# Storing the two halves of each weight next to each other, word by word, so that a weight load steps over every second word

## The chip, the cores and the metric

One NeuronCore of a Trainium2 chip runs the whole program in one launch. The time is device microseconds of one execution. The engines are named as the profile names them: PE is TensorE's matmul stream, PEld its weight loads, DVE is VectorE, ACT is ScalarE, POOL is GpSimd, SP the engine that issues DMAs.

## What is computed

Three blocks in a row on 256 tokens of width 1024: two layers of (feed-forward, a mixer of three recurrent kinds, feed-forward), and a block with attention, a convolution and a feed-forward with a convolution in it. Nearly all arithmetic is in dense products `x @ w` in float32; cut to what matters here:

```python
def swiglu(x, w_gate_up, w_down):                      # widths 1024 -> 2 x 2816 -> 1024
    gate, up = jnp.split(x @ w_gate_up, 2, axis=-1)
    return (jax.nn.silu(gate) * up) @ w_down
...
x = x + FFN_HALF * swiglu(rms_norm(x, g1), ...)        # first feed-forward of a layer
x = x + mixers(rms_norm(x, g2) @ w_in) @ w_out         # ssd, mlstm, rwkv heads
x = x + FFN_HALF * swiglu(rms_norm(x, g3), ...)        # second feed-forward of a layer
...
x = x + gt1 * (mixed @ w_out)                          # last block: attention and convolution
x = x + gt2 * ((silu(gte) * val) @ w_down)             # last block: feed-forward
```

## The kernel before, in words

All weights of the dense products lie in DRAM as one stream `ws` of 3,808 blocks of 128 x 128 in the order in which they are used, 7 blocks to a chunk (`CB`), 544 chunks. A chunk passes through three steps. `fetch` (lines 121 to 124) loads it with one DMA into a `raw` tile (128 x 896 float32, 6 buffers). `chunk` (lines 126 to 136) lets ACT round it into a tile `whi` of the type fp32r (line 134), and lets DVE subtract the rounded value from the raw one into a second tile `wlo` (line 135); each has 4 buffers. `mm` (lines 151 to 155) then does three matmuls for every block: rounded weights by rounded activations (153), rounded weights by the activations' remainder (154), remainder of the weights by rounded activations (155). Weights are the side that is loaded into the array, 128 columns; the streamed side is 256 tokens (258 in the first groups of the last block). So there are 3 x 3,808 = 11,424 dense matmuls, each with a weight load of its own, and a chunk serves 21 of them.

The activations are kept as two fp32r tiles as well: `pair0` and `pair1` (16 KB a partition, halves 8 KB apart) for inputs of width 1024, `hp` for the inner width of a feed-forward, `xg` for two groups that start before a norm is known. `split` (lines 204 to 206) makes them with the same two operations.

A feed-forward (`ffn`, line 321 on) is 22 steps of two output tiles of 8 blocks each (gate and up), and then the down projection over 22 blocks for each of 8 output tiles. On the profile's clock the five down projections run at about 136 to 195, 598 to 657, 782 to 845, 1242 to 1305 and 1550 to 1615 us, the gate and up parts before them at 23 to 136, 486 to 598, 670 to 781, 1131 to 1242 and 1436 to 1550 us (the last one with a convolution, `taps3`, after each product). Between 195 and 486 and between 845 and 1131 us stand the mixers, with many small float32 matmuls, and from 1305 to 1436 us attention.

The order of instructions on each engine is made by a scheduler from the order in which the code issues them and from priorities; the weight copies have a high one (`tc.high_priority(AHEAD)`). Semaphores follow from the tiles: the first matmul on a chunk waits for ACT, the third for DVE, ACT waits until a buffer is no longer read.

`gap` (lines 258 to 261) allocates a tile that nothing reads and has POOL fill it; its only effect is to move the tiles that are allocated after it. `GAPS` (line 41) holds its sizes in bytes a partition. With them, in the built program, every `whi` and `wlo` buffer begins at byte 416 of a 512-byte period (a block is 512 bytes wide, so every block does), `pair0` at 96, `pair1` at 352, and the five `hp` tiles, in the order of the down projections above, at 96, 352, 160, 32 and 288.

Three more lines are named below. Line 221 is the sum over channels for a norm: weights 128 x 128, one streamed column. Line 671 is an ACT pass of 256 elements that reads a tile once by columns (a step of 64 bytes) and once by rows; line 617 a DVE pass of 256 elements that writes with a step of 128 bytes. Lines 1215 and 1216 are float32 matmuls of attention, 64 weight columns and 128 streamed ones, in two passes each.

Of the kernel before, what the change touches and what calls it, by code (L numbers as in the profile page):

```python
# [8 lines left out]
F32 = mybir.dt.float32  # L9
F32R = mybir.dt.float32r  # L10
# [17 lines left out]
CB = 7  # L28
NB = 4
# [8 lines left out]
GD_AHEAD = 1  # L38
BOOST = (1, 1, 1, 1, 1)
DENSE = 0.34  # L40
GAPS = {"xg": 448, "xn": 192, "mix": 288, "ffn": (384, 128, 448, 192, 448), "attn": 256}
W_OUT = ((("rwkv0", "rwkv1"), (12, 13, 14, 15)), (("ssd",), (0, 1, 2, 3, 4, 5, 6, 7)), (("mlstm",), (8, 9, 10, 11)))

IN_PAIRS = "k0 r0 v0 r2 k2 v2 xb8 xb0 dtg xb2 xb4 xb6 z0 z2 z4 xm0 z6 xm2 o0 o2".split()
# [33 lines left out]
def _program(tc, a, order, dbg=None):  # L78
# [3 lines left out]
    V, S, G, PE = nc.vector, nc.scalar, nc.gpsimd, nc.tensor  # L82

    def pool(name, bufs=1, **kw):
        return es.enter_context(tc.tile_pool(name=name, bufs=bufs, **kw))

    const = pool("const")
    wp = pool("weights")
# [30 lines left out]
    chunks, raws = {}, {}  # L119

    def fetch(ci):
        if ci not in raws and ci < N_CHUNKS:
            raws[ci] = wp.tile([128, CB * 128], F32, name="raw", bufs=NR)
            nc.sync.dma_start(raws[ci], a["ws"][ci])

    def chunk(ci):
        if ci in chunks or ci >= N_CHUNKS:
            return
        fetch(ci)
        raw = raws[ci]  # L130
        hi = wp.tile([128, CB * 128], F32R, name="whi", bufs=NB)
        lo = wp.tile([128, CB * 128], F32R, name="wlo", bufs=NB)
        with tc.high_priority(AHEAD):
            S.copy(hi, raw)  # L134
            V.tensor_sub(lo, raw, hi.bitcast(F32))  # L135
        chunks[ci] = (hi, lo)

    def block(mat, l, k, m):
        i = len(order)
        order.append((mat, l, k, m))  # L140
        ci, b = divmod(i, CB)
        for c in range(ci, ci + NB):
            chunk(c)
        for c in range(ci, ci + NR):
            fetch(c)
        hi, lo = chunks[ci]
        if b == CB - 1:
            del chunks[ci - 1 if ci - 1 in chunks else ci]
        return hi[:, b * 128:b * 128 + 128], lo[:, b * 128:b * 128 + 128]
# [92 lines left out]
    def stat_rstd(accs, width, eps, chain=False):  # L242
# [9 lines left out]
            S.copy(rb, p2[:, i * T:(i + 1) * T])  # L252
            out.append(rb)
        return out

    turn = []

    def gap(pool, n):
        if n:
            turn.append(0)  # L260
            G.memset(pool.tile([128, n // 4], F32, name=f"gap{len(turn)}"), 0.0)

    pairs = []

    def pair(dtype=F32R):
        pairs.append(0)
        return act.tile([128, 2, DT, T], dtype, name=f"pair{len(pairs) % 2}")
# [4 lines left out]
    def new_acc():  # L272
        return act.tile([128, 2, T], F32, name="acc", bufs=2)
# [47 lines left out]
    def ffn(l, which, acc, xg, next_gain):  # L321
        with tc.tile_pool(name=f"ffn{which}{l}", bufs=1) as fp:
            gu, dn = f"ffn{which}_w_gate_up", f"ffn{which}_w_down"
            gap(fp, GAPS["ffn"][2 * l + which - 1])
            hp = fp.tile([128, 2, FT, T], F32R, name="hp")
            rb, = stat_rstd([acc], D, EPS)
# [58 lines left out]
    def mixers(l, acc, xg):  # L385
# [6 lines left out]
        def weight(i):  # L392
            w = ring(128, 512)
            nc.sync.dma_start(w, a["small"][l, i])
            return w

        gap(mp, GAPS["mix"])
        nka = mp.tile([128, 4], F32, name="nka")
        V.tensor_scalar(nka, P(f"k_a{l}", 0, 4), -1.0, None, op0=OP.mult)
# [739 lines left out]
    def modulate(rb, gain, shift):  # L1139
        xn = pair()  # L1140
        for j in range(DT):
            n = tmp()[:, 0]
            V.scalar_tensor_tensor(n, x[:, j], gain[:, j:j + 1], rb, op0=OP.mult, op1=OP.mult)
            S.activation(xn[:, 0, j], n, AF.Identity, bias=shift[:, j:j + 1])
            V.scalar_tensor_tensor(xn[:, 1, j], n, shift[:, j:j + 1], xn[:, 0, j].bitcast(F32),
                                   op0=OP.add, op1=OP.subtract)
        return xn
# [12 lines left out]
    def second(accs, xg):  # L1160
        rb, rb2 = stat_rstd(accs, D, EPS, chain=True)
        with tc.tile_pool(name="attn", bufs=1) as mp:
            xn = modulate(rb2, a1[:, 0], mod[:, 0:8])
            gap(mp, GAPS["attn"])
            mixed = [mp.tile([128, 2, 4, T], F32R, name=f"m{i}") for i in range(2)]
            at, cv = (mp.tile([128, 4, T], F32, name=n) for n in ("at", "cv"))
# [101 lines left out]
        with tc.tile_pool(name="ffn_2", bufs=1) as fp:  # L1268
            rb, = stat_rstd([acc], D, EPS)
            xn = modulate(rb, a1[:, 1], mod[:, 24:32])  # L1270
            gap(fp, GAPS["ffn"][4])
            hp = fp.tile([128, 2, FT, T], F32R, name="hp")
# [40 lines left out]
    acc = new_acc()  # L1313
    gap(act, GAPS["xg"])
    xg = pair()
    gap(act, GAPS["xn"])
    for j in range(0, DT, 2):
        nc.sync.dma_start(x[:, j:j + 2], a["xT"][:, j:j + 2])
        gained((j, j + 1), xg, "ffn1_norm0")
        chunk(j // 2)  # L1320
# [6 lines left out]
    for l in range(LAYERS):  # L1327
        acc, xg = ffn(l, 1, acc, xg, f"mix_norm{l}")
        dbg(f"xa{l}", x)
        acc, xg = mixers(l, acc, xg)  # L1330
# [4 lines left out]
        acc, xg = ffn(l, 2, acc, xg, f"ffn1_norm{l + 1}" if l + 1 < LAYERS else None)  # L1335
# [162 lines left out]
```

## Time and profile before

| what | value |
|---|---|
| median of 2 runs | 1624.52 us (1621.25 to 1627.79) |
| the profiled execution | 1627.1 us |
| its span, first to last instruction | 1625.3 us |
| mean granted clock of TensorE | 0.989 |
| busy share PE, PEld, DVE, ACT, POOL | 98%, 93%, 71%, 62%, 3% |
| DMA: HBM read, mean rate over the span | 287.51 MB, 178 GB/s |

Busy shares count an engine as busy while any row of it runs. Matmul rows are pipelined: a row lasts from its issue to the end of its last column, and the next begins before that, so the share of PE says that matmuls follow each other without a pause, and not how fast they follow. The pace is read from start times in the timeline, or from the number of matmuls in a stretch. The windows view gives for a stretch, from the span's start in us, the busy time of each engine and the number of its instructions that overlap the stretch (x), the granted clock of TensorE as a share of 2.4 GHz, and the DMA engines' share and rate.

### The profile page before, as it was taken

Reading aid. Unit: us, or ns where it says so; the run is one execution under the profiler, and the core shown is the slowest. Engines: PE = TensorE matmul, PEld = TensorE weight load, DVE = VectorE, ACT = ScalarE, POOL = GpSimd, SP = SyncE. Lnnn points to the kernel's source line nnn. Section 1 sums busy time; section 2 is a strip of 40 time slices with the busy share of each in tenths; the row PEclk is TensorE's granted clock in tenths of the full one; section 3 lists DMA queues with packets and bytes.
Section 4 is the critical chain, followed back from the end, with each engine's and each line's share of the span. In section 5 each row is a group of like instructions: output and inputs, shape, how many; then the busy total and the mean of one; then the engine's idle time right before and its main releaser. Section 6 shows DMA issues by size and latency. Waiting matters only on the chain.

```text
span 1625.3 us, 33775 instructions
## 1 busy us (share of the span) xinstructions
PE 1584.9 (98%) x13660; PEld 1516.4 (93%) x13660; DVE 1161.4 (71%) x1965; ACT 1000.1 (62%) x1692; POOL 47.5 (3%) x68
## 2 busy tenths in 40 slices
PE   8999999999999999999999899999999999999998
PEld 7999988878999999999998887799999998999997
DVE  7865679856787755787568975688785676798853
ACT  6554576887655454545458788765554566587753
POOL 0000001000000000000000100000000000000000
PEclk9999989999999999999999999999999999999999
DMA  7866633333357766597563333436886653556662
GB/s 252 306 195 190 204 118 123 101 112 116 115 181 244 242 187 194 185 329 260 183 194 125 115 106 117 127 117 216 288 306 185 185 166 113 159 162 190 187 189 72
DMA packets 106717, 290.81 MB, mean 179 GB/s; under 512 B 15640, under 2 KB 28096, under 8 KB 106432
## 3 DMA queue, kind: packets, MB, share of 16 engines
q1 hardware_dynamic: 106272, 288.12, 55.9%
q8 instruction: 107, 1.75, 0.4%
q10 hardware_dynamic: 288, 0.52, 0.1%
q14 instruction: 50, 0.41, 0.1%
HBM read 287.51 MB, written 1.09 MB: 178 GB/s over the span
## 4 chain that ended last, share of the span: by engine, by line
PE 77%; issue 13%; DVE 5%; ACT 2%; DMA 1%; POOL 1%; SPq 0%; DVEq 0%; POOLq 0%; ACTq 0%
PE d L155 21%; PE d L153 21%; PE d L154 21%; DVE wlo L135 1%; DMA ada<-ada 1%; PE m L691 1%; PE m L754 1%; PE m L1064 1%; POOL stm L212 1%; PE m L1068 1%; PE m L736 1%; PE st L221 1%; PE m L705 1%; ACT whi L134 1%; PE m L1066 1%
## 5 line engine op out<-in xcount | busy, mean ns | idle before, releaser
L135 DVE TENSOR_TENSOR wlo<-raw,whi 128x896 fp32r<-128x896 f32 x544 | 590.4, 1089 | 245.1 <-ACT whi L134 242.3
L153 PE MATMUL d<-pair,whi 128*128 128x256 f32 x2672 | 753.2, 282 | 4.8 <-ACT whi L134 2.1
L155 PE MATMUL d<-pair,wlo 128*128 128x256 f32 x2672 | 753.8, 282 | 1.8 <-DVE wlo L135 1.8
L154 PE MATMUL d<-pair,whi 128*128 128x256 f32 x2672 | 752.9, 282 | 0.1
L134 ACT CAST whi<-raw 128x896 fp32r<-128x896 f32 x544 | 511.5, 943 | 348.3 <-PE d L154 254.0
L153 PEld LDWEIGHTS d<-pair,whi 128*128 128x128 f32 x2672 | 508.8, 190 | 14.8 <-issue 5.9
L155 PEld LDWEIGHTS d<-pair,wlo 128*128 128x128 f32 x2672 | 508.1, 190 | 7.2 <-DVE wlo L135 2.9
L154 PEld LDWEIGHTS d<-pair,whi 128*128 128x128 f32 x2672 | 508.5, 190 | 3.0 <-issue 1.4
L154 PE MATMUL d<-hp,whi 128*128 128x256 f32 x880 | 246.6, 280 | 0.0
L155 PE MATMUL d<-hp,wlo 128*128 128x256 f32 x880 | 246.1, 280 | 0.0
L153 PE MATMUL d<-hp,whi 128*128 128x256 f32 x880 | 246.1, 280 | 0.0
L155 PEld LDWEIGHTS d<-hp,wlo 128*128 128x128 f32 x880 | 166.2, 189 | 0.0
L154 PEld LDWEIGHTS d<-hp,whi 128*128 128x128 f32 x880 | 166.1, 189 | 0.0
L153 PEld LDWEIGHTS d<-hp,whi 128*128 128x128 f32 x880 | 166.1, 189 | 0.0
L205 ACT CAST hp<-h 128x256 fp32r<-128x256 f32 x88 | 35.4, 406 | 90.9 <-DVE h L345 90.8
L1124 DVE SCALAR_TENSOR_TENSOR adasum<-ada,sc,adasum 128x1024 f32<-128x1024 f32 x42 | 53.8, 1281 | 14.4 <-DMA ada<-ada 14.4
L206 DVE TENSOR_TENSOR hp<-h,hp 128x256 fp32r<-128x256 f32 x88 | 36.7, 421 | 15.3 <-ACT hp L205 14.5
L1157 DVE SCALAR_TENSOR_TENSOR up<-raw,par,up 128x255 f32<-128x255 f32 (+1 forms) x88 | 37.2, 480 | 10.6 <-ACT raw L1153 10.3
L344 ACT ACTIVATE s<-d 128x256 f32<-128x256 f32 x80 | 30.2, 378 | 23.3 <-PE d L155 22.2
L345 DVE TENSOR_TENSOR h<-s,d 128x256 f32<-128x256 f32 x88 | 36.0, 415 | 3.8 <-ACT s L344 3.8
L155 PE MATMUL d<-w,wlo 128*128 128x256 f32 x128 | 37.1, 290 | 0.0
L154 PE MATMUL d<-w,whi 128*128 128x256 f32 x128 | 37.1, 290 | 0.0
(403 smaller groups left out, 1829.0 us busy)
## 6 DMA issues: line engine op xcount, KB each, us to landing
raw<-ws SPq DMA_DIRECT2D x544, 448.0 KB, 3.7
ada<-ada SPq DMA_DIRECT2D x48, 512.0 KB, 5.9
w<-da SPq DMA_DIRECT2D x16, 256.0 KB, 5.1
w<-small SPq DMA_DIRECT2D x10, 256.0 KB, 3.9
ab<-abias SPq DMA_DIRECT2D x1, 1536.0 KB, 7.1
x<-xT SPq DMA_DIRECT2D x4, 256.0 KB, 4.9
w<-da SPq DMA_DIRECT2D x8, 128.0 KB, 3.6
w<-dw SPq DMA_DIRECT2D x4, 256.0 KB, 5.5
```

Of the source, the lines that this page charges most:

```text
L134: S.copy(hi, raw)
L135: V.tensor_sub(lo, raw, hi.bitcast(F32))
L153: PE.matmul(p, h, xh, start=start, stop=False, skip_group_check=True)
L154: PE.matmul(p, h, xl, start=False, stop=False, skip_group_check=True)
L155: PE.matmul(p, lo, xh, start=False, stop=stop, skip_group_check=True)
L205: S.copy(hi, src)
L206: V.tensor_sub(lo, src, hi.bitcast(F32))
L212: G.tensor_tensor(dst, m, mhalf.to_broadcast([128, n]), op=OP.pow)
L344: S.activation(s, p[:, 0], AF.Silu)
L345: V.tensor_mul(h, s, p[:, 1])
L1124: V.scalar_tensor_tensor(acc, w, sc[:, k:k + 1], acc, op0=OP.mult, op1=OP.add)
L1157: V.scalar_tensor_tensor(dst[:, i, d:], raw[:, i, :T - d], P(w, 3 * j + k), dst[:, i, d:], op0=OP.mult, op1=OP.add)
```

## The change

The two tiles `whi` and `wlo` of a chunk become one tile `wsp` of 128 x 896 x 2: word 0 of each pair is the rounded value, word 1 the remainder. `hi` and `lo` are views of it with a step of two words (8 bytes). ACT and DVE write through these views, DVE reads `hi` through one, and the weight loads read them. A buffer has 7,168 bytes, as the two had together, and there are 4 as before. The sizes of the gap tiles are other ones, and there is a new gap ahead of the first weight buffer; `gap` itself moves up in the code without a change.

```diff
-GAPS = {"xg": 448, "xn": 192, "mix": 288, "ffn": (384, 128, 448, 192, 448), "attn": 256}
+GAPS = {"w": 96, "xg": 64, "xn": 64, "mix": 32, "ffn": (0, 64, 192, 0, 64), "attn": 0}
...
     def chunk(ci):
         if ci in chunks or ci >= N_CHUNKS:
             return
         fetch(ci)
         raw = raws[ci]
-        hi = wp.tile([128, CB * 128], F32R, name="whi", bufs=NB)
-        lo = wp.tile([128, CB * 128], F32R, name="wlo", bufs=NB)
+        if not chunks:
+            gap(wp, GAPS["w"] * (not order))
+        w = wp.tile([128, CB * 128, 2], F32R, name="wsp", bufs=NB)
+        hi, lo = w[:, :, 0], w[:, :, 1]
         with tc.high_priority(AHEAD):
             S.copy(hi, raw)
             V.tensor_sub(lo, raw, hi.bitcast(F32))
```

In the built program every `wsp` buffer begins at a multiple of 1,024 bytes, and a block is 1,024 bytes wide. In the 512-byte period `pair0` now begins at 192, `pair1` at 64, and the five `hp` tiles at 320, 384, 0, 448 and 0. Each engine has as many instructions as before, but POOL, which fills two gap tiles fewer. The scheduler orders a few of them otherwise. Lines 126 to 262 stand 9 further down in the new file, later ones 2.

On DVE, in the gate and up part of the last feed-forward (1436 to 1550 us before), L135 is the subtraction for a chunk, L1157 the convolution, L1287 the product of the two halves, L206 the remainder of the activations. Before:

```order
1438 L135 TENSOR_TENSOR wlo<-raw,whi 128x896
1439 L206 TENSOR_TENSOR hp<-up,hp 128x256
1440 L1157 SCALAR_TENSOR_TENSOR up<-raw,par,up 128x255 x2
1441 L1157 SCALAR_TENSOR_TENSOR up<-raw,par,up 128x254 x2
1442 L135 TENSOR_TENSOR wlo<-raw,whi 128x896
1443 L1287 TENSOR_TENSOR up<-up 128x256
1444 L135 TENSOR_TENSOR wlo<-raw,whi 128x896
1445 L206 TENSOR_TENSOR hp<-up,hp 128x256
1446 L135 TENSOR_TENSOR wlo<-raw,whi 128x896
```

And now, at the same place (L144 is L135, L215 L206, L1159 L1157, L1289 L1287):

```order
1442 L144 TENSOR_TENSOR wsp<-raw,wsp 128x896
1443 L215 TENSOR_TENSOR hp<-up,hp 128x256
1444 L1159 SCALAR_TENSOR_TENSOR up<-raw,par,up 128x255 x2
1445 L1159 SCALAR_TENSOR_TENSOR up<-raw,par,up 128x254 x2
1446 L144 TENSOR_TENSOR wsp<-raw,wsp 128x896 x2
1447 L1289 TENSOR_TENSOR up<-up 128x256
1448 L144 TENSOR_TENSOR wsp<-raw,wsp 128x896
1449 L215 TENSOR_TENSOR hp<-up,hp 128x256
```

One subtraction for a coming chunk moves ahead of the product of the halves by three places; the number of each kind is the same. On POOL, from the program's start, the gap tiles are filled in the same places (`gap` and the number of a tile; L212 is the root of a norm). Before:

```order
6 L261 MEMSET gap_88 128x112
7 L261 MEMSET gap_91 128x48
8 L261 MEMSET gap_153 128x96
9 L212 ISA
10 L212 TENSOR_TENSOR stm<-stm,mhalf 128x2
11 L261 MEMSET gap_2471 128x72
```

Now:

```order
6 L131 MEMSET gap_88 128x16
7 L131 MEMSET gap_91 128x16
8 L131 MEMSET gap_100 128x24
9 L221 ISA
10 L221 TENSOR_TENSOR stm<-stm,mhalf 128x2
11 L131 MEMSET gap_2392 128x8
```

The fills are smaller; the third one is that ahead of the weight buffers, where that of the first feed-forward stood.

## Rows read from the trace of the kernel before

**Rows 1.** The page: busy us, share of the span, instructions.
```profile
PE 1584.9 (98%) x13660; PEld 1516.4 (93%) x13660; DVE 1161.4 (71%) x1965; ACT 1000.1 (62%) x1692; POOL 47.5 (3%) x68
```
**Rows 2.** The page: the chain that ended last, by engine and by line.
```profile
PE 77%; issue 13%; DVE 5%; ACT 2%; DMA 1%; POOL 1%; SPq 0%; DVEq 0%; POOLq 0%; ACTq 0%
PE d L155 21%; PE d L153 21%; PE d L154 21%; DVE wlo L135 1%; DMA ada<-ada 1%; PE m L691 1%; PE m L754 1%; PE m L1064 1%; POOL stm L212 1%; PE m L1068 1%; PE m L736 1%; PE st L221 1%; PE m L705 1%; ACT whi L134 1%; PE m L1066 1%
```
**Rows 3.** Timeline of PEld, 137.0 to 137.6 us: start us, length us, instruction.
```profile
136.98 0.19 PEld L154 LDWEIGHTS d<-hp,whi 128*128 128x128 f32 x1
137.09 0.19 PEld L155 LDWEIGHTS d<-hp,wlo 128*128 128x128 f32 x1
137.21 0.19 PEld L153 LDWEIGHTS d<-hp,whi 128*128 128x128 f32 x1
```
**Rows 4.** Timeline of PE, same stretch.
```profile
136.98 0.28 PE L153 MATMUL d<-hp,whi 128*128 128x256 f32 x1
137.09 0.28 PE L154 MATMUL d<-hp,whi 128*128 128x256 f32 x1
137.21 0.28 PE L155 MATMUL d<-hp,wlo 128*128 128x256 f32 x1
```
**Rows 5.** Timeline of PEld, 16.1 to 17.0 us.
```profile
16.17 0.98 PEld L221 LDWEIGHTS st<-ones,acc 128*128 128x128 f32 x8
```
**Rows 6.** Timeline of PE, 1372.0 to 1372.8 us.
```profile
1372.11 0.38 PE L1215 MATMUL m<-sT,vn 128*64 128x128 f32 x2
1372.33 0.38 PE L1216 MATMUL m<-sT,vn 128*64 128x128 f32 x2
```
**Rows 7.** Windows: stretch, its length, busy us (x count) by engine, clock, DMA.
```profile
23.00:136.00 113.00, 111.73 (x978) 110.36 (x977) 79.99 (x110) 58.70 (x94) 0.00 (x0) 1.00 0.73 237
136.00:195.00 59.00, 59.00 (x523) 59.00 (x522) 34.83 (x42) 28.78 (x38) 0.00 (x0) 1.00 0.63 195
670.00:781.00 111.00, 110.97 (x979) 109.64 (x978) 84.66 (x113) 57.18 (x93) 0.00 (x0) 1.00 0.79 267
782.00:845.00 63.00, 63.00 (x528) 63.00 (x527) 34.90 (x42) 29.01 (x39) 0.00 (x0) 1.00 0.59 183
1242.00:1305.00 63.00, 63.00 (x533) 63.00 (x533) 37.39 (x47) 31.54 (x46) 0.00 (x0) 1.00 0.61 184
1436.00:1550.00 114.00, 113.54 (x964) 113.33 (x963) 100.81 (x185) 89.95 (x162) 0.00 (x0) 1.00 0.60 185
1550.00:1615.00 65.00, 65.00 (x543) 64.16 (x542) 32.58 (x42) 28.29 (x40) 0.00 (x0) 1.00 0.42 128
...
441.00:461.00 20.00, 20.00 (x174) 20.00 (x173) 13.25 (x17) 8.99 (x12) 2.47 (x1) 1.00 0.55 168
```
**Rows 8.** Lines L671, L617 and L206: shortest, median, longest ns.
```profile
L671 ACT ACTIVATE w<-w,cst x16: 493/622/759, 280.5 to 976.2; 128x256 f32<-128x256 f32 x16
...
L617 DVE TENSOR_TENSOR w<-am,cst x16: 577/601/631, 249.3 to 929.4; 32x256 f32<-32x256 f32 x16
...
L206 DVE TENSOR_TENSOR hp<-h,hp x88: 415/420/428, 32.0 to 1245.6; 128x256 fp32r<-128x256 f32 x88
```
**Rows 9.** The page: groups of instructions, busy us, mean ns, idle time before them.
```profile
L135 DVE TENSOR_TENSOR wlo<-raw,whi 128x896 fp32r<-128x896 f32 x544 | 590.4, 1089 | 245.1 <-ACT whi L134 242.3
...
L134 ACT CAST whi<-raw 128x896 fp32r<-128x896 f32 x544 | 511.5, 943 | 348.3 <-PE d L154 254.0
```
**Rows 10.** Waits: who waited for whom, us in total, times, longest us.
```profile
ACT whi L134 <- PE d L154: 254.0, 203, 5.0
```

More of the change, by code (lines that the diff above doesn't have):

```diff
@@ L124, in fetch, with gap @@
             nc.sync.dma_start(raws[ci], a["ws"][ci])
+    turn = []
+    def gap(pool, n):
+        if n:
+            turn.append(0)
+            G.memset(pool.tile([128, n // 4], F32, name=f"gap{len(turn)}"), 0.0)
     def chunk(ci):
@@ L254, in stat_rstd @@
         return out
[L256 to L261, printed above, removed]
     pairs = []
```

## Prediction

> **What bounds the kernel now.** I read the page's busy shares first: the matmul row of TensorE (PE) covers 98% of the span, VectorE (DVE) 71%, ScalarE (ACT) 62% [rows 1]. The chain that ended last agrees: 77% of the span is PE, the three matmul lines of `mm` are the first three entries with 21% each, and the DVE pass that makes the remainder half appears with 1% [rows 2]. So the rate of the 11,424 dense matmuls (3 for each of 3,808 weight blocks) is the time, and all else matters only where it stops that rate.
>
> The busy row does not tell the rate, since a matmul row is 0.28 us long and the next one starts long before it ends. The timeline does: matmuls start 0.11 to 0.12 us apart, each weight load (PEld) starts within 0.01 us of the matmul before its own, and the matmul it feeds starts when 0.11 us have gone by [rows 3, 4]. Is it the load or the streaming of 256 columns that takes the 0.11 us? Two other places answer. In the statistics (L221) the streamed side is a single column and the weights are 128 wide as here: 8 loads take 0.98 us, the last of them 0.19, so 7 steps of 0.79/7 = 113 ns [rows 5]. Loads alone come no faster than here. Where the weights are 64 wide and the streaming is 128 columns of plain fp32 in two passes, two steps take 0.22 us, 110 ns each [rows 6]. Streaming alone needs nearly as much, so a shorter load would win 3 ns at most. The load sits in the loop, by a hair.
>
> The windows view gives the rate by stage. A window counts every matmul that overlaps it, so about 2.4 (0.28 us of row at 0.113 spacing) are counted too many. In 136 to 195 us: 59.0 / (523 - 2.4) = 113.3 ns. In 782 to 845 us, the same down projection in the next layer, same lines and shapes: 63.0 / 525.6 = 119.9 ns. In 1242 to 1305 it is 118.7, in 1550 to 1615 it is 120.2, in 1436 to 1550 (113.54 busy) it is 118.1, and in 441 to 461 116.6 [rows 7]. The granted clock is 1.00, the upper level of 2.4 GHz, in all of these. The instructions don't differ; what differs is where the activations lie in SBUF against the weight buffers (the addresses stand under the change). So there is a disturbance between the two reads of TensorE that depends on addresses, worth 0 to 7 ns a matmul.
>
> **The change part by part.** *The load with a step of two words.* It still reads 128 words, but over 1,024 bytes and not 512. The 256 streamed columns are 1,024 bytes too. Both reads begin together and last about as long [rows 3, 4]; today the load moves through its addresses at half the speed of the stream, so the distance between the two changes during each matmul, and after the change it stays nearly constant. I expect that to remove most of the disturbance, and the floor of 113.3 ns to stay, since loads alone don't go faster [rows 5]. What is there to win, stage by stage, as busy time less (count - 2.4) x 0.1133: 1.2 us in 23 to 136, 0 in 136 to 195, 0.3 in 670 to 781, 3.4 in 782 to 845, 2.9 in 1242 to 1305, 4.6 in 1436 to 1550, 3.7 in 1550 to 1615, together 16.1 us for 5,031 matmuls [rows 7]. The other 6,393 matmuls lie in stages like 23 to 136 and 670 to 781 (1.5 us for 1,952, 0.8 ns each) and in mixers and attention, of which 441 to 461 is a sample with 3.2 ns. By the first rate they hold 5 us, by the second 20. I take 5, the rate of the longer stretches: 21 us in all, at most 37.
>
> No row shows a weight load with a step. From below: it cannot gain more than the 3.3 ns down to 110, 11,424 x 3.3 = 38 us beyond the 21. From above: the nearest rows are ACT's copies that read with a step of 64 bytes, 759 ns against 493 for 256 elements [rows 8], 1.04 ns an element. A load with that price on 128 columns would take 133 ns longer, and the kernel 1.5 ms longer. Between these I take no change of the load itself, because 8 bytes are far nearer to 4 than to 64.
>
> *The split writes.* ACT's rounding (544 x 943 ns) and DVE's subtraction (544 x 1,089 ns) [rows 9] now write every second word, and DVE reads its second operand so. Order and waits hold: the scheduler still waits for ACT before the first matmul of a chunk and for DVE before the third, the two halves being tracked apart. Price from below: 0. From above: ACT at 1.04 ns an element (64-byte step), +0.93 us a chunk; DVE at the price of L617, which writes with a step of 128 bytes, 601 ns against 420 for a contiguous pass of 256 elements [rows 8], 0.71 ns an element, +0.63 us a chunk. I take 0, again for the nearness of 8 bytes to 4. Cover if I am wrong: ACT waits 254 us in 203 waits for a free weight buffer [rows 10], so the halves are made well ahead, and DVE has 33.0 us free in 23 to 136 for about 47 chunks, 0.7 each. Least cover is in 1436 to 1550: DVE 100.81 and ACT 89.95 of 114 [rows 7], for 964/21 = 46 chunks: 0.29 us a chunk on DVE, 0.52 on ACT.
>
> On such steps the Trainium skill holds two rules that differ. "SBUF — State Buffer", section "Door 1: The DMA port swizzle", says that accesses stay at full speed while at least two fall on the same 16-byte line: a step of 8 bytes is then free, and the sum stands. "Vector Engine (DVE) Microarchitecture Reference", section "5.2 Measured stream behaviour on trn2", wants runs of two adjacent words, and lists 2.50 ns a column, against 1.05, for an output that steps 24 words. By that figure, an estimate, L135 would cost 1.3 us more, DVE 707 us more in all, and it would bound the kernel near 1,870 us; rival (d) is this rule, priced by rows. No run here shows a step of 8 bytes; L617 at 128 bytes costs 0.71 ns more, half of that page's extra.
>
> *Order and the gaps.* The scheduler moves a few instructions by one to three places on DVE and ACT and swaps matmul groups in the mixers; nothing is added, and DMA issues keep their number. The weight copies were already free to go ahead by several chunks, so I cost this at 0, within 3 us either way. The POOL fills of the gap tiles shrink; they wait for PE and nobody waits for them.
>
> **The sum.** The profiled execution took 1627.1 us. Less 21: 1606. The median shown is 2.6 us below that execution, so 1603.5, say 1603, 1.3% below before. I call a change of over 2% faster or slower, about what a measurement here can tell from none.
>
> **The rivals.**
> (a) *The load leaves the loop.* If the step lets the load end early, the stream falls to the 110 ns of the fp32 pairs [rows 6]: 38 us more, 1603 - 38 = 1565; half of it gives 1584. For it: the load row ends what the matmul waits for [rows 3, 4]. Against: streaming has only 3 ns to give.
> (b) *The stream does not care.* The disturbance is bound to the addresses of lines and banks and stays on average: 1624.
> (c) *Every address is bad.* The load touches twice as many bytes and so meets the stream twice as often; all matmuls run at the 119.9 ns of 782 to 845. Today's mean is 113.3 + 21,000/11,424 = 115.1, so 11,424 x 4.8 ns = 55 us: 1679, slower. It decides wherever the average passes 118. For it: three down projections at 118.7 to 120.2 show how lasting such a state is; and the new addresses against the weights differ from stage to stage. Against: a constant distance can be bad only as long as the slower side has not slipped out of the way.
> (d) *The split writes cost what rows 8 show.* In 1436 to 1550 DVE needs 100.81 + 46 x 0.63 = 129.8 us of 114, ACT 89.95 + 46 x 0.93 = 132.7: +19. In 670 to 781 DVE has 84.66 + 47 x 0.63 = 114.3 of 111: +3; 1131 to 1242, a like stage, the same. Peaks in the mixers do not average out; I add 10. That is 1624 + 35 = 1659 with nothing gained on PE, 1643 with the gain of the other stages. It decides from 0.29 us a chunk on.
>
> **How the numbers follow.** Forecast 0.47 (its own range 1592 to 1612), (a) 0.17, (b) 0.13, (c) 0.12, (d) 0.11. Two per cent is 1592 below and 1657 above. Faster: most of (a) and the tail of the forecast, 0.22. Slower: most of (c), half of (d) and the dear loads, 0.19. Within 2%: 0.59. The range leaves out the lower end of (a) and the upper part of (c): 1575 to 1662.
>
> **What would show it.** Right: the two passes over the weights stay at 0.94 and 1.09 us; the windows of the five down projections all show 113 to 114 ns; the loads of L221 are unchanged; DVE and ACT idle as before. Wrong: spacing under 112 anywhere (a); a mean of 115 or more with other stages at 118 to 120 (b, c); L135's successor above 1.4 us and PE waiting for it in the last feed-forward (d); weight load rows of 0.3 us would mean that a stepped load is dear by itself.

## The result, and the profile after

The changed kernel takes 1672.13 us (median of 2 runs, 1671.33 and 1672.94) against 1624.52 before: ratio 1.0293, 95% interval 1.0201 to 1.0385. It is slower, by 48 us. The forecast was 1603, and its range ended at 1662.

The page of the kernel after: busy time by engine, the chain that ended last, and the groups that answer to [rows 1, 2, 9].

```profile
PE 1631.0 (98%) x13660; PEld 1564.8 (94%) x13660; DVE 1165.5 (70%) x1965; ACT 1044.6 (63%) x1692; POOL 46.8 (3%) x66
...
PE 77%; issue 13%; DVE 4%; ACT 4%; POOL 1%; DMA 0%; POOLq 0%; DVEq 0%; SPq 0%; ACTq 0%
...
L144 DVE TENSOR_TENSOR wsp<-raw,wsp 128x896 fp32r<-128x896 f32 x544 | 591.9, 1092 | 290.1 <-ACT wsp L143 286.8
L143 ACT CAST wsp<-raw 128x896 fp32r<-128x896 f32 x544 | 557.7, 1028 | 374.2 <-PE d L164 267.6
...
L162 PEld LDWEIGHTS d<-pair,wsp 128*128 128x128 f32 x2672 | 522.5, 196 | 13.0 <-issue 4.8
```

The group of weight loads that L162 answers to, on the page before:

```profile
L153 PEld LDWEIGHTS d<-pair,whi 128*128 128x128 f32 x2672 | 508.8, 190 | 14.8 <-issue 5.9
```

The chain is as before: 77% PE. The two passes over the weights are not what grew into the path. DVE's subtraction takes 1,092 ns against 1,089; ACT's rounding takes 1,028 against 943, but ACT still waits 267.6 us for a free weight buffer (254.0 before), so it runs ahead as it did. The load row grew from 190 to 196 ns, and PE's busy time by 46 us, which is the loss.

The rate is read as before, from starts in the timeline. PE in the first down projection, which [rows 4] showed before the change:

```profile
145.73 0.28 PE L163 MATMUL d<-hp,wsp 128*128 128x256 f32 x1
145.85 0.28 PE L164 MATMUL d<-hp,wsp 128*128 128x256 f32 x1
145.97 0.29 PE L162 MATMUL d<-hp,wsp 128*128 128x256 f32 x1
146.10 0.28 PE L163 MATMUL d<-hp,wsp 128*128 128x256 f32 x1
```

Three steps take 0.37 us here; before, two took 0.23. The windows view over the stretches that answer to [rows 7], in the same order (stretch, length, busy us and count by engine, clock, DMA):

```profile
23.00:136.00 113.00, 111.50 (x925) 110.28 (x924) 75.81 (x104) 59.05 (x88) 0.00 (x0) 1.00 0.70 228
142.00:201.00 59.00, 59.00 (x487) 59.00 (x487) 32.99 (x41) 29.11 (x37) 0.00 (x0) 1.00 0.58 181
690.00:801.00 111.00, 111.00 (x925) 110.18 (x925) 81.82 (x107) 58.23 (x87) 0.00 (x0) 1.00 0.76 258
809.00:871.00 62.00, 62.00 (x519) 62.00 (x519) 34.67 (x42) 30.35 (x37) 0.00 (x0) 1.00 0.59 183
1279.00:1341.00 62.00, 62.00 (x519) 62.00 (x518) 36.33 (x46) 32.63 (x44) 0.00 (x0) 1.00 0.60 182
1480.00:1594.00 114.00, 113.56 (x947) 113.35 (x945) 99.08 (x181) 92.07 (x161) 0.00 (x0) 1.00 0.60 182
1596.00:1660.00 64.00, 63.68 (x523) 62.58 (x522) 31.13 (x39) 28.75 (x37) 0.00 (x0) 1.00 0.40 125
```

Busy time over (count - 2.4) gives 120.9, 121.8, 120.3, 120.0, 120.0, 120.2 and 122.3 ns. (In the last stretch small matmuls stand among the dense ones, each time with some steps of 150 ns and more; between neighbouring dense ones the starts are 120.0 apart. The same holds for the last of [rows 7], which had 120.2: by starts it is 118.8.) By starts the seven stood between 113.3 and 119.9 before and stand between 120.0 and 121.7 now. So the stages that were fast have gone, and each runs at the pace of the slowest one before, or just above. The clock is 1.00 in all.

Over the whole program, the starts of neighbouring dense matmuls (those less than 130 ns apart, some 10,900) lie 115.3 ns apart before and 120.2 after. Times 11,424 the difference is 56 us; the span grew by 45.8 (1625.3 to 1671.1). Some 10 come back, and most of that shows in the two mixers, from the first dense matmul behind one feed-forward to the first of the next. Before:

```profile
196.50:473.88 277.38, 267.15 (x2339) 241.19 (x2339) 207.45 (x427) 204.02 (x368) 18.29 (x23) 0.96 0.41 125
846.02:1118.88 272.86, 262.81 (x2339) 237.99 (x2339) 207.18 (x427) 203.92 (x368) 18.30 (x23) 0.98 0.42 127
```

After:

```profile
206.19:482.85 276.66, 266.44 (x2340) 241.99 (x2340) 208.20 (x427) 208.50 (x368) 18.17 (x22) 0.99 0.41 125
871.69:1147.44 275.75, 266.24 (x2340) 241.68 (x2340) 208.03 (x427) 208.74 (x368) 18.20 (x23) 0.99 0.42 125
```

Together the mixers grew by 2.2 us, though each holds 1,368 dense matmuls, worth 6.7 us at 4.9 ns. The granted clock in them was 0.96 and 0.98 before and is 0.99 after: windows laid around the stretches at the lower level show 0.50 for some 31 us before and 7 us after. At half the pace 24 us hold 12 us of work at the full one, an estimate; the difference to be explained in the mixers is 11. Counted over the whole program, neighbouring dense matmuls that start 130 ns or more apart were 316 (74.3 us in all) and are 261 (62.9 us). That is 11 us less, and not all of it is the clock's, since many of these steps stand right behind a small float32 matmul. These sums compare one execution with one; the 19 executions of the kernel before in the first batch of experiments lie between 1620.5 and 1635.6 us, a spread as large as what comes back. Why the clock falls less often after the change stays open. It works against the loss and doesn't explain it.

### The profile page after: what moved, and what is told of

The parts are those of the page before. It is cut to its first block, busy times and chain, and to the rows that moved or that the text cites. A ratio compares the mean times of both kernels' runs of the same rounds, so it can differ in the third digit from the quotient of the medians.

```text
span 1671.1 us, 33750 instructions
## 1 busy us (share of the span) xinstructions
PE 1631.0 (98%) x13660; PEld 1564.8 (94%) x13660; DVE 1165.5 (70%) x1965; ACT 1044.6 (63%) x1692; POOL 46.8 (3%) x66
## 4 chain that ended last, share of the span: by engine, by line
PE 77%; issue 13%; DVE 4%; ACT 4%; POOL 1%; DMA 0%; POOLq 0%; DVEq 0%; SPq 0%; ACTq 0%
PE d L162 21%; PE d L164 21%; PE d L163 21%; DVE wsp L144 1%; ACT wsp L143 1%; PE m L693 1%; PE m L756 1%; PE m L1066 1%; PE m L1070 1%; POOL stm L221 1%; PE st L230 1%; PE m L707 1%; PE m L1068 1%; PE m L738 1%; PE m L162 0%
## 5 line engine op out<-in xcount | busy, mean ns | idle before, releaser
L144 DVE TENSOR_TENSOR wsp<-raw,wsp 128x896 fp32r<-128x896 f32 x544 | 591.9, 1092 | 290.1 <-ACT wsp L143 286.8
L143 ACT CAST wsp<-raw 128x896 fp32r<-128x896 f32 x544 | 557.7, 1028 | 374.2 <-PE d L164 267.6
L162 PE MATMUL d<-pair,wsp 128*128 128x256 f32 x2672 | 763.1, 286 | 3.8 <-ACT wsp L143 2.1
L164 PE MATMUL d<-pair,wsp 128*128 128x256 f32 x2672 | 762.5, 286 | 1.5 <-DVE wsp L144 1.5
L163 PE MATMUL d<-pair,wsp 128*128 128x256 f32 x2672 | 761.7, 285 | 0.4 <-DVE pair L215 0.3
L162 PEld LDWEIGHTS d<-pair,wsp 128*128 128x128 f32 x2672 | 522.5, 196 | 13.0 <-issue 4.8
L164 PEld LDWEIGHTS d<-pair,wsp 128*128 128x128 f32 x2672 | 522.3, 196 | 7.3 <-issue 3.7
L163 PEld LDWEIGHTS d<-pair,wsp 128*128 128x128 f32 x2672 | 523.3, 196 | 2.9 <-DVE pair L215 0.5
L163 PE MATMUL d<-hp,wsp 128*128 128x256 f32 x880 | 249.4, 283 | 0.3 <-DVE hp L215 0.3
L164 PE MATMUL d<-hp,wsp 128*128 128x256 f32 x880 | 249.7, 284 | 0.0
L162 PE MATMUL d<-hp,wsp 128*128 128x256 f32 x880 | 248.8, 283 | 0.0
L162 PEld LDWEIGHTS d<-hp,wsp 128*128 128x128 f32 x880 | 172.3, 196 | 0.0
L163 PEld LDWEIGHTS d<-hp,wsp 128*128 128x128 f32 x880 | 171.4, 195 | 0.5 <-DVE hp L215 0.5
L164 PEld LDWEIGHTS d<-hp,wsp 128*128 128x128 f32 x880 | 171.6, 195 | 0.0
L215 DVE TENSOR_TENSOR hp<-h,hp 128x256 fp32r<-128x256 f32 x88 | 36.7, 421 | 12.1 <-ACT hp L214 11.3
L1159 DVE SCALAR_TENSOR_TENSOR up<-raw,par,up 128x255 f32<-128x255 f32 (+1 forms) x88 | 37.2, 479 | 10.2 <-ACT raw L1155 9.9
L163 PE MATMUL d<-w,wsp 128*128 128x256 f32 x128 | 37.6, 294 | 0.0
L164 PE MATMUL d<-w,wsp 128*128 128x256 f32 x128 | 37.4, 292 | 0.0
```

The source lines that it names most:

```text
L162: PE.matmul(p, h, xh, start=start, stop=False, skip_group_check=True)
L163: PE.matmul(p, h, xl, start=False, stop=False, skip_group_check=True)
L164: PE.matmul(p, lo, xh, start=False, stop=stop, skip_group_check=True)
L215: V.tensor_sub(lo, src, hi.bitcast(F32))
L1159: V.scalar_tensor_tensor(dst[:, i, d:], raw[:, i, :T - d], P(w, 3 * j + k), dst[:, i, d:], op0=OP.mult, op1=OP.add)
```

## The experiments

Theory A says that a weight load with a step of two words is slower by itself. Rival B says that only its meeting with the stream is, so that the addresses decide. Rival C is the new set of gaps, rival D the split writes. (These capitals are not the prediction's rivals (a) to (d).) All kernels but the two made of repeated groups are the changed kernel with the edit shown, except where it says otherwise; ratios are to the kernel before, run beside them.

**undo_layout.** The gaps of the change, the two tiles of before.

```diff
-        w = wp.tile([128, CB * 128, 2], F32R, name="wsp", bufs=NB)
-        hi, lo = w[:, :, 0], w[:, :, 1]
+        hi = wp.tile([128, CB * 128], F32R, name="whi", bufs=NB)
+        lo = wp.tile([128, CB * 128], F32R, name="wlo", bufs=NB)
```

> The changed kernel with its gap sizes, but whi and wlo again two tiles read with a step of one word; everything else, addresses of the activations too, is as in the changed kernel. A: the stream goes back to 113 to 118 ns, 1600 to 1630 us. B: as the places fall out, between 1603 and 1679. C: 1672, as the changed kernel.

Measured: 1632.25 us, ratio 1.0019 (0.9996 to 1.0042), a little above the 1630 that A allowed, beside a kernel before at 1629.52 in this batch. The loss is in the layout. C falls. The new gaps aren't quite free: by starts the mean spacing here is 116.2 ns, against 115.3 in the kernel before.

**by_block.** One tile, but each block's two halves behind each other: the tile, its size and the 1,024 bytes from block to block stay, the step goes.

```diff
-        w = wp.tile([128, CB * 128, 2], F32R, name="wsp", bufs=NB)
+        w = wp.tile([128, CB, 2, 128], F32R, name="wsp", bufs=NB)
         hi, lo = w[:, :, 0], w[:, :, 1]
...
-            S.copy(hi, raw)
-            V.tensor_sub(lo, raw, hi.bitcast(F32))
+            r3 = raw.rearrange("p (b i) -> p b i", b=CB)
+            S.copy(hi, r3)
+            V.tensor_sub(lo, r3, hi.bitcast(F32))
...
-        return hi[:, b * 128:b * 128 + 128], lo[:, b * 128:b * 128 + 128]
+        return hi[:, b], lo[:, b]
```

> The changed kernel with the two halves in one tile, next to each other block by block (128 rounded words, then 128 remainder words): one tile and a block pitch of 1,024 bytes as in the changed kernel, but loads and writes with a step of one word. A: like undo_layout, 1600 to 1630 us. B: as the places fall out. C, or a loss by the one tile: 1672.

Measured: 1633.96 us, ratio 1.0031 (1.0005 to 1.0057), again just above A's range. One tile instead of two costs next to nothing; what is left is the step.

**shift_32.** The weights lie 32 bytes further down against the activations.

```diff
-GAPS = {"w": 96, "xg": 64, ...
+GAPS = {"w": 64, "xg": 96, ...
```

> The changed kernel, step of two words, with the weight buffers 32 bytes further down and all activations where they were (gap w 64, xg 96). A: 1672 and 120 ns everywhere, as the changed kernel. B: another disturbance, towards 113 ns and 1603 us in some of the stages, or different by stage. C: about 1672 less or more by a few us.

Measured: 1671.96 us, ratio 1.0267 (1.0234 to 1.0300). A shift of 32 bytes, which moves a step-1 load to another pace (below, steps_and_places), changes nothing that can be measured here; the mean spacing is 120.1 ns. So B can't mean a bad address any more; that the stepped load meets the stream everywhere isn't ruled out yet.

**writes_stepped and loads_stepped** do one half of the change each. In the first the passes write every second word and the loads read in one stretch:

```diff
-        chunks[ci] = (hi, lo)
+        f = w.rearrange("p i h -> p (i h)")
+        chunks[ci] = (f[:, :CB * 128], f[:, CB * 128:])
```

> The two passes write every second word, as in the change; the weight loads read each chunk's tile in two stretches, step 1. So the loads don't get the halves that were written, and the products differ from the reference's; each chunk's first matmul now waits for both passes. Theory A (the step of the load is the loss): 1632 to 1636 us, the time of undo_layout and by_block, ratio 1.002 to 1.006; the two passes stay at 1.03 us (ScalarE) and 1.09 us (VectorE). Rival D (the stepped writes cost: ScalarE's 85 ns more a pass, or writes that get in the way of TensorE's reads): 1672, ratio 1.025 or more; a part of the loss in between.

In the second it is the other way round:

```diff
-        hi, lo = w[:, :, 0], w[:, :, 1]
+        f = w.rearrange("p i h -> p (i h)")
+        hi, lo = f[:, :CB * 128], f[:, CB * 128:]
...
-        chunks[ci] = (hi, lo)
+        chunks[ci] = (w[:, :, 0], w[:, :, 1])
```

> The reverse: the passes write each half in one stretch of the tile, step 1, and the loads read every second word of it. The products differ from the reference's, as before, and each chunk's first matmul waits for both passes. Theory A: the whole loss, 1668 to 1676 us, ratio 1.025 to 1.030, a mean spacing of 120; ScalarE's pass back at 943 ns. Rival D: 1632 to 1636, ratio 1.002 to 1.006.

Measured: writes_stepped 1638.19 us, ratio 1.0065 (1.0038 to 1.0092); loads_stepped 1668.09, ratio 1.0256 (1.0229 to 1.0283). The groups of the first (busy us, mean ns, idle time before them and its releasers):

```profile
L143 ACT CAST wsp<-raw 128x896 fp32r<-128x896 f32 x544 | 552.8, 1019 | 336.4 <-PE d L165 245.8 <-issue 48.6 <-ACT wsp L143 15.8
L163 PEld LDWEIGHTS d<-pair,wsp 128*128 128x128 f32 x2672 | 507.6, 190 | 20.0 <-DVE wsp L144 8.5 <-issue 5.3 <-DVE h L348 2.6
```

and of the second:

```profile
L144 ACT CAST wsp<-raw 128x896 fp32r<-128x896 f32 x544 | 511.7, 942 | 399.9 <-PE d L165 284.1 <-issue 84.2 <-ACT hp L215 4.8
L163 PEld LDWEIGHTS d<-pair,wsp 128*128 128x128 f32 x2672 | 522.2, 196 | 14.8 <-issue 4.8 <-ACT wsp L144 3.9 <-DVE h L348 1.8
```

With stepped loads alone the load row is at 196 ns, the mean spacing at 120.2 and the time where the full change has it; ACT is back at 942 and that helps nothing. With stepped writes alone ACT has 76 of its 85 ns more, the load row stands at 190 and the mean spacing at 116.5 (by_block 116.0). The 1.0065 is a little over the expected 1.006. Part of it belongs to this experiment, since each chunk's first load now waits for both passes (8.5 us for DVE, L144); the interval still meets that of by_block. At most a few us are the writes': D falls as the main cause.

**half_stepped.** Odd chunks keep the step, even ones do not.

```diff
-        hi, lo = w[:, :, 0], w[:, :, 1]
+        if ci % 2:
+            hi, lo = w[:, :, 0], w[:, :, 1]
+        else:
+            f = w.rearrange("p i h -> p (i h)")
+            hi, lo = f[:, :CB * 128], f[:, CB * 128:]
```

> Every second chunk keeps the step of two words; in the others each half lies in one stretch of the same tile, step 1. Theory A (each stepped load pays for itself): half of the loss, between the 1632.25 of undo_layout and the 1671.96 of shift_32, so 1652 us, ratio 1.014 to 1.017 to the kernel before; spacings in the trace of 120 in odd chunks and 113 to 118 in even ones. Rival S (a stepped load puts the two reads out of step, and the slow pace then lasts, as the stretches of 118 in the kernel before last over hundreds of matmuls): 120 in nearly all chunks, over 1665, ratio 1.023 or more.

Measured: 1650.96 us, ratio 1.0164 (1.0130 to 1.0199), about half of the loss. The timeline of PEld shows the two paces side by side; the rows are the second loads of four chunks in a row, 21 loads apart, the first and third of them in odd chunks:

```profile
42.27 0.20 PEld L167 LDWEIGHTS d<-pair,wsp 128*128 128x128 f32 x1
...
44.79 0.19 PEld L167 LDWEIGHTS d<-pair,wsp 128*128 128x128 f32 x1
...
47.18 0.20 PEld L167 LDWEIGHTS d<-pair,wsp 128*128 128x128 f32 x1
...
49.70 0.19 PEld L167 LDWEIGHTS d<-pair,wsp 128*128 128x128 f32 x1
```

21 loads take 2.52 us, then 2.39, then 2.52: 120.0, 113.8 and 120.0 ns each. Over the program the mean is 120.4 within odd chunks and 115.6 within even ones. The price is paid load by load, and no slow pace outlasts a chunk. Rival S falls.

**steps_and_places** computes nothing of the reference: it repeats loads and matmuls in groups of 189, from weights that lie with a step of 1, 2, 4 or 8 words (`kone`, `ktwo`, `kfour`, `keight`), and rounds and subtracts into these tiles.

```python
for reps: for b in range(7):       # weight blocks of 128
    matmul(p, hi[block b], x); matmul(p, hi[block b], x); matmul(p, lo[block b], x)
```

> This kernel computes nothing of the reference: it measures weight loads by themselves, in groups of 189 matmuls with the kernel's sequence (rounded, rounded, remainder; 7 blocks), weights stored with a step of 1, 2, 4 or 8 words, 2, 320 or 512 streamed columns, and then 256 columns from 16 places in SBUF, 32 bytes apart in a 512-byte period. Theory A (a stepped load is slower by itself): with 2 columns 112 ns at step 1 and about 119 at step 2; with 256 columns 120 at step 2 in all 16 places; with 320 and 512 columns no difference between the steps (about 136 and 216 ns). Theory B (two reads disturb each other, by address): with 2 columns 112 ns at both steps; with 256 columns some places at 113 and others at 118 to 120, at both steps, so a good place for step 2 exists. Theory C (the new gap sizes): step 1 and step 2 alike in every group.

Windows within groups of 256 columns: step 1 at the same place as the weights (modulo 256 bytes), step 1 at 192 bytes behind them, then steps 2, 4 and 8 at the first place:

```profile
525.50:546.50 21.00, 21.00 (x178) 21.00 (x177) 0.00 (x0) 0.00 (x0) 0.00 (x0) 1.00 0.01 2
662.00:683.00 21.00, 21.00 (x187) 20.94 (x185) 0.00 (x0) 0.00 (x0) 0.00 (x0) 1.00 0.01 2
888.00:909.00 21.00, 21.00 (x177) 21.00 (x177) 0.00 (x0) 0.00 (x0) 0.00 (x0) 1.00 0.00 1
1256.00:1299.00 43.00, 43.00 (x186) 43.00 (x186) 0.00 (x0) 0.00 (x0) 0.00 (x0) 1.00 0.00 1
1969.00:2011.00 42.00, 42.00 (x176) 42.00 (x176) 0.00 (x0) 0.00 (x0) 0.00 (x0) 1.00 0.00 1
```

By starts (the mean of each group, without the first few) these are 120.0, 113.3, 120.0, 233.3 and 241.7 ns. Over 16 places 32 bytes apart, step 1 gives 113.3 at one distance of eight (192) and 117.3 to 120.0 at the others, the same for distances that differ by 256; step 2 gives 120.0 to 121.1 at all of them. So in the change the address matters hardly any more, at a price. The kernel undo_layout shows the same map: its five down projections lie at 64, 128, 0, 192 and 0 and run at 117.8, 118.7, 120.0, 113.4 and 119.9 ns by starts; the groups of step 1 have 117.8, 118.6, 120.0 and 113.3 at 64, 128, 0 and 192.

With more columns A was partly right. At 320, steps 1 and 2 take 146.7 ns both, where it had said 136; at 512 they take 226.9 and 233.3, where it had said 216 and no difference. At 512 a stepped load of less than 120 ns has time to spare, so beside its own time it also slows the stream that it meets there.

The groups with 2 columns were to show the load alone, but the granted clock fell to 0.50 in them, as these windows in the groups of steps 2 and 4 show:

```profile
70.00:100.00 30.00, 30.00 (x142) 30.00 (x142) 0.00 (x0) 0.00 (x0) 0.00 (x0) 0.50 0.00 1
110.00:150.00 40.00, 40.00 (x173) 40.00 (x173) 0.00 (x0) 0.00 (x0) 0.00 (x0) 0.50 0.00 0
```

At 213 ns a load steps 1 and 2 can't be told apart at that clock. Step 4 took 233.3 ns in it, no more than at 1.00. So the price of a wide step doesn't follow TensorE's clock, the load's own time does (213 ns here, 111.5 at the upper level in the next kernel), and the longer of the two counts. For the load alone at the upper level a second kernel was made:

**loads_alone**, made in the same way, puts only 21 matmuls with 2 columns behind 63 dense ones, and adds a step of 3.

> This kernel computes nothing of the reference; its weight loads and matmuls are repeated in groups and only its profile is read. Weights lie with a step of 1, 2, 3 or 4 words; the streamed tile has 2 columns (21 matmuls at a time, behind 63 dense ones, so that the clock is still at its upper level), then 128, 160, 192, 224, 240, 256 and 264 columns at two places, and 256 columns of step 1 at places 8 bytes apart. Measured in steps_and_places with dense groups: 113 to 120 ns from start to start at step 1, 120 at step 2, 233 at step 4, 240 to 244 at step 8: the price grows with the bytes spanned up to 4 words and then no more. Theory A (the load by itself pays for every stretch of 16 bytes that it touches, 233/128 = 1.82 ns each, beside its own 111.7): alone, with 2 columns, 112 ns at step 1, 117 to 120 at step 2, 175 to 180 at step 3, 233 at step 4, and the same with 128 to 224 columns. Theory B (a stepped load is as fast as another, and only loses against the stream that it meets): alone 112 at step 2 as at step 1, and rising with the columns to 120 at 256; at step 3 no more than 125. For the places 8 bytes apart I have one expectation: 113.3 only in a stretch of 32 bytes or less around the one good place, 117 to 120 elsewhere.

Timeline of PEld, the first and the last of the 21 loads of a group for steps 1, 2, 3 and 4 (start, length):

```profile
39.56 0.19 PEld L55 LDWEIGHTS d<-xb,kone 128*128 128x128 f32 x1 [0.25 <-PE d L57]
...
41.79 0.19 PEld L57 LDWEIGHTS d<-xb,kone 128*128 128x128 f32 x1
...
74.66 0.19 PEld L55 LDWEIGHTS d<-xb,ktwo 128*128 128x128 f32 x1 [0.32 <-issue]
...
77.01 0.20 PEld L57 LDWEIGHTS d<-xb,ktwo 128*128 128x128 f32 x1
...
108.66 0.25 PEld L55 LDWEIGHTS d<-xb,kthree 128*128 128x128 f32 x1 [0.32 <-issue]
...
112.16 0.26 PEld L57 LDWEIGHTS d<-xb,kthree 128*128 128x128 f32 x1
...
149.01 0.31 PEld L55 LDWEIGHTS d<-xb,kfour 128*128 128x128 f32 x1 [0.32 <-issue]
...
153.67 0.33 PEld L57 LDWEIGHTS d<-xb,kfour 128*128 128x128 f32 x1
```

Over 20 steps: 2.23 us, 2.35, 3.50 and 4.66, so 111.5, 117.5, 175 and 233 ns a load, with next to nothing streamed and the clock at 1.00 in these windows. That is theory A, number for number. With 128, 160, 192, 224 and 240 columns at the same place as the weights, all at a clock of 1.00, the means are 111.7 at step 1 all through, and 117.8, 117.8, 118.8, 119.0 and 120.0 at step 2; with 256 columns 120.0 at both. (Some groups at the other place and of step 3 fell to a clock of 0.50; there step 3 takes 213 ns as well.) So 6 ns are the stepped load's own, and its meeting with the stream adds up to 2.5 at this place. Against the 113.3 of a good place, where load and stream together take 2 ns more than the load alone, a stepped load costs 6.7 at 256 columns: 4.2 by itself and 2.5 by the meeting. Against the worst place it costs nothing. Twelve further places of step 1 at 256 columns, 8, 16 and 24 bytes behind four of the 32-byte ones around the good one, give 116.7 to 122.7, so the fast distance is a single one, inside the 32 bytes that I had expected; above my 120 lie 121.4 and 122.7. These twelve also begin off the 32-byte grid on which all other places lie, and no run tells that from the distance.

**good_places.** The kernel before, with activations of all five down projections at the fast distance.

```diff
-GAPS = {"xg": 448, "xn": 192, "mix": 288, "ffn": (384, 128, 448, 192, 448), "attn": 256}
+GAPS = {"xg": 448, "xn": 192, "mix": 288, "ffn": (384, 128, 384, 256, 512), "attn": 256}
```

> The kernel before, with three gap lengths changed (384, 256 and 512 in place of 448, 192 and 448), so that the activations of all five down projections lie 192 bytes behind the weights, counted modulo 256, as those of the two fast ones did. Theory P (this distance sets the pace of a step-1 load): the three down projections that took 120.0, 118.7 and 118.8 ns a matmul take 113.3, so 527 x (6.6 + 5.4 + 5.5) = 9.2 us less than the kernel before, some 1615 us, ratio 0.994. Rival Q (the pace is set by something else that differs between stages, and the place only happens to go with it): 1624, ratio 1.000 within 0.002. The up projection of the last feed-forward, which had 117.8 at the good distance, may stay or fall to 113.3 by either; that would be 4 us more.

Measured: 1617.49 us against 1625.53 before, ratio 0.9956 (0.9935 to 0.9978), the fastest kernel of this study. Windows in the five down projections:

```profile
136.00:195.00 59.00, 59.00 (x524) 59.00 (x522) 34.34 (x42) 28.75 (x37) 0.00 (x0) 1.00 0.64 195
594.00:652.00 58.00, 58.00 (x514) 58.00 (x513) 34.28 (x41) 27.47 (x36) 0.00 (x0) 1.00 0.64 197
780.00:837.00 57.00, 57.00 (x506) 57.00 (x505) 33.39 (x40) 27.74 (x37) 0.00 (x0) 1.00 0.63 194
1240.00:1297.00 57.00, 57.00 (x505) 57.00 (x504) 35.10 (x44) 29.98 (x42) 0.00 (x0) 1.00 0.62 190
1543.00:1603.00 60.00, 59.92 (x518) 58.88 (x518) 30.37 (x38) 25.59 (x35) 0.00 (x0) 1.00 0.41 130
```

59 / 521.6, 58 / 511.6, 57 / 503.6, 57 / 502.6: 113.1 to 113.4 ns, and the fifth at 113.9 by starts. The three that had 118.6 to 119.9 by starts before are cured: P holds. The up projections were not touched and moved both ways by starts: that of the last feed-forward from 117.8 to 114.0, two others from 113.6 to 115.4. They lie at the fast distance all the time, so at that distance there is a second pace; what brings it about is open and wasn't tried.

## Why the prediction was wrong

*What bounds the kernel* held. The matmuls are the time, the load sits in the loop "by a hair", and little but their rate changed. "By a hair" was close: loads alone take 111.5 ns, load and stream together 113.3 at best. Order and gaps stayed within the 3 us allowed for them by the time (1632.25 against 1629.52 in undo_layout); by spacing the new places are 0.9 ns a matmul worse for a step of one word. One reading was off: the 120.2 of 1550 to 1615 counts small matmuls' time as the dense ones'; by starts it is 118.8, and the 3.7 us to be won there are some 0.8 too many.

*The load with a step of two words* is the step that failed, at "between these I take no change of the load itself, because 8 bytes are far nearer to 4 than to 64". It measured 117.5 ns alone against 111.5, and 120.2 on average among the kernel's matmuls against 115.3. The nearness in bytes was the wrong scale. Steps 2, 3 and 4 cost 117.5, 175 and 233 ns, 64, 96 and 128 times 1.82 to 1.84 ns, and step 8 hardly more than step 4 (240 to 244 among dense matmuls): that fits a price for each stretch of 16 bytes that the load touches. At step 1 it touches 32, which would be 58 ns, well under the 111.5 that the load takes anyway. So the price isn't a small part of a large penalty; it is hidden until it passes the load's own time, and at two words it just does. The groups at a clock of 0.50 bear that out: with its own time at 213 ns, a load pays nothing for steps 2 and 3. The measured +6 lies between my bounds of -3.3 and +133, but I put the term at nothing. Since the load had less than 2 ns to spare, a twentieth of the upper bound was enough to turn the sign. My sign for a dear load, rows of 0.3 us, was set far too high: the rows went from 190 to 196 ns.

"I expect that to remove most of the disturbance" came half true, in the half that gains nothing: the pace hardly depends on the address any more (120.0 to 121.1 over all places), but it is that of the worst place. The 21 us to be won were not there, and nearly 7 ns a load were added to the stages that had been at 113.3, 48 us in all: that makes the 69 between 1603 and 1672. The loads of L221, which the change doesn't touch, take 0.98 us for eight as in [rows 5].

Rival (c) had the right number, all at 119.9 and 1679, but in the main for another reason. It said that the load meets the stream twice as often. loads_alone shows the load slow with 2 columns streamed, half_stepped shows it load by load, and the meeting adds some 2.5 ns to that. Its 55 us were the 56 that the spacing shows; it came out 7 us too long, and in the profiled executions some 10 came back, at least in part through the clock. Rival (b), 1624, fell with the result, in which every stage moved to 120 and more. Rival (a) fell with the stepped load's 117.5 alone; at 256 columns no place gave less than 113.3.

*The split writes* were costed at 0, and that was right for the time. The passes took 3 ns more on DVE and 85 on ACT, far within the 0.52 us a chunk that ACT had to spare in the tightest stage, and writes_stepped lies some 0.3% over by_block, its own longer wait included. Rival (d) falls: its prices, 0.63 and 0.93 us a chunk, were those of far larger steps.

On the two rules of the Trainium skill weighed there: DVE's 1,092 ns show that the one of "Vector Engine (DVE) Microarchitecture Reference", "5.2 Measured stream behaviour on trn2", on pairs of adjacent words, does not show at a step of two. The Trainium skill's "SBUF — State Buffer" ("Door 1: The DMA port swizzle") says that two accesses to a 16-byte line give full speed; DVE agrees, TensorE's load does not, and ACT's copy, 1,028 ns against 943, does not either. For TensorE the fit above gives a reason: two words in 1.82 ns are 0.91 ns each, and the load takes one in 111.5 / 128 = 0.87. By the rows below DVE takes 1,866 / 896 = 2.08 ns a word at a step of four, so two words to a stretch would be 1.04 each, and at a step of one it takes 1.25: time enough. ACT doesn't fit this: 1,838 / 896 = 2.05 ns would be 1.03 a word, under the 1.06 of its step of one, and yet it pays for two words.

## What to carry to other kernels

For TensorE's load and for DVE a layout was free here as long as reading it stayed faster than the engine takes the words; ACT paid sooner. So price the step for the engine that sits in the loop, not for the one that writes, and measure that instruction alone in a kernel of twenty lines before changing a real one. Where an instruction on the path has next to no slack, "nearly free" is not a term that can be set to zero. And where equal stages run at two paces, the distance between the two operands in memory is worth a look: three gap lengths gave 0.4% here.

## What the runs showed that was not expected

The price of a step differs by engine and nearly stops growing at a step of 16 bytes. steps_and_places, groups of DVE and ACT, nearly all of them before TensorE's stream began (busy us, mean ns):

```profile
L46 DVE TENSOR_TENSOR keight<-raw,keight 128x896 fp32r<-128x896 f32 x3 | 5.7, 1885 | 0.0
L46 DVE TENSOR_TENSOR kfour<-raw,kfour 128x896 fp32r<-128x896 f32 x3 | 5.6, 1866 | 0.0
L46 DVE TENSOR_TENSOR ktwo<-raw,ktwo 128x896 fp32r<-128x896 f32 x3 | 3.4, 1118 | 0.0
L46 DVE TENSOR_TENSOR kone<-raw,kone 128x896 fp32r<-128x896 f32 x3 | 3.4, 1118 | 0.0
```

```profile
L45 ACT CAST kfour<-raw 128x896 fp32r<-128x896 f32 x3 | 5.5, 1838 | 0.1
L45 ACT CAST ktwo<-raw 128x896 fp32r<-128x896 f32 x3 | 3.1, 1022 | 0.0
L45 ACT CAST kone<-raw 128x896 fp32r<-128x896 f32 x3 | 2.8, 949 | 0.0
```

DVE pays nothing at two words and 67% at four; ACT 8% and 94%. So 73 of ACT's 85 ns in the kernel are its own and not a collision with TensorE.

A matmul of 256 columns has its fast pace of 113.3 ns at one distance between activations and weights (192 modulo 256 bytes); 8 bytes aside, on either side, it is at 120. With 240 columns and step 1 the pace at the bad place is 111.7, at 256 it is 120.0: the last 16 columns cost 8 ns.
